# Setting back a planner's count of owed vector work: a two-layer Hyena and attention trunk on one core

## The chip, the core and the metric

The kernel runs on one core of a Trainium2 chip. Its engines are TensorE (PE in the profile, PEld for its weight loads), VectorE (DVE), ScalarE (ACT), GpSimd (POOL) and SyncE (SP, which only issues loads here). The metric is the device time of one execution in microseconds (us), as the median of several runs of the same program.

## The reference

Two layers. Each is a feed-forward, a mixer and another feed-forward, with a residual around each part:

```python
x = x + 0.5 * swiglu(rms_norm(x, ffn1_norm[l]), ...)
h = rms_norm(x, mix_norm[l])
x = x + hybrid_mixer(h, ...)
x = x + 0.5 * swiglu(rms_norm(x, ffn2_norm[l]), ...)
```

x is 256 positions by 1024 channels in float32, and a feed-forward is 2688 wide. The mixer has two branches, merged by gates. One is Hyena: three convolved projections of 512 channels, then twice `z = x_o * (k_o (*) z + D_o z)`, where `(*)` is a long convolution done by a Fourier transform and D_o is a skip weight per channel. The filters k_o come from a small network that depends on the layer's weights only, not on x:

```python
hid = jnp.sin(z @ w1 + b1)
hid = jnp.sin(hid @ w2 + b2)
k = (hid @ w3).reshape(L, HY_ORDER, 2, HY_WIDTH)
k = k * jnp.exp(-t * deltas[None])[:, None, None, :]
full = concatenate([k[:, :, 0], zeros, k[:0:-1, :, 1]])
full = full * lax.rsqrt(jnp.sum(full * full, axis=0) + EPS)
return jnp.fft.rfft(full, axis=0)
```

The other branch is attention in three groups of four heads, with a norm of queries and keys.

## The kernel before

**Weights.** Every matmul with weights is done as three products: each operand is split into a rounded part and the rest. A weight chunk is 128 rows by 1024 float32 (512 KB). `loads` (line 137) lets SP fetch it into one of four `raw` buffers, `pump_hi` (145) lets ACT round it into `whi`, and `pump_lo` (155) lets DVE write the rest, `wlo` (1024 elements a partition). Seven pairs of `whi` and `wlo` exist. The list `srcs` (from line 105) holds the chunks in the order of their use, and SP's queue issues them in that order.

**Slots.** The whole program is written out in one order by hand, and each engine does its part of it in that order. The unit is a slot (236): the matmuls of one weight chunk, usually 24 of 256 columns. Before them a slot lets side work go (`tick`, 211) and flushes what the slot before left (`retire`, 171: a new rounding on ACT, the evacuation if one is due, a new `wlo` on DVE).

**Side work** is written as Python generators that stop at `yield`: the filters and, in layer 0, tables of constants during the first feed-forward; the query and key norms, Hyena and attention during the mixer. A tick takes steps of them as long as the count `owed` is under the stage's room. `ROOM` gives 0.9 for the convolution's slots of the mixer, 2.2 and 2.5 for its later ones, and 1.5 for the feed-forwards. A step that yields True has started something that must come back from another engine. It may go on only when the count at that moment, at most 4.86, has run down to 0.2 (`await_`, 208). The transposes of the convolution (`trans`) and of an opening's result (`turn`) stand in a list of their own, `urgent`, under the same due time but without the room.

**The count** stands for DVE work that is written but not done. Each counted DVE operation adds 0.07 and 1.04e-3 for each element of a partition, and each slot takes off 2.43:

```python
def counted(f):
    def g(**kw):
        owed[0] += OVER + 1.04e-3 * math.prod(kw["out"].shape[1:])
        return f(**kw)
...
def passed(t):
    owed[0] = max(0.0, owed[0] - t)
```

So a `wlo` adds 1.135, an operation on 512 elements 0.602 and one on 256 elements 0.336. The groups at a stage's end and the first half of an opening don't call `passed`.

**Stages.** Each layer has three stages that begin with an `opening` (351). It does four weight chunks first for the even positions (j=0), beside the norm of the odd ones, and then again as four slots for j=1. There are six in all. After it, the first feed-forward runs chunks m=2 to m=20, two slots each (gate and up), with three `acc` banks of PSUM; the evacuation of a chunk is a tanh on ACT and three DVE operations. Then `proj_out` (374) follows. The mixer's opening is followed by six convolution chunks (`conv`, two slots each), the rest of the queries, keys and values, eight gates of two slots, and four merges.

**The filters** (547): a matmul `s<-fc`, a sine (seven DVE operations and an ACT sine), a second matmul `s<-sd`, a second sine, then `st`. For each of the two filters the generator then sets `want` and waits for `fw3_unit` (533), which the feed-forward calls behind chunk m of `FW3`: eight matmuls of the third weights on `st`. If the generator isn't there yet, `fw3_unit` takes its steps one after the other with no matmuls between (`drain`, 248). What follows a unit is one chain: `k`, `sq`, transposes of `sq` and of `rb`, the factor `nb`, the skip row, `hl`, a Fourier matmul, `spec`.

**The first query norm** (`qknorm`, 866) of the mixer: a square on ACT and a reduce on DVE for each half, a scale `ss` on DVE, a power on POOL (`rs`), the product `qk` by `rs` on DVE, and four transposes on PE for each half.

Of the kernel before, what the change touches and what calls it, by code (L numbers as in the profile page):

```python
# [37 lines left out]
ROOM = (0.9, 2.2, 2.5, 1.5, 1.5)  # L38
OVER = 0.07
MARGIN = 0.2  # L40
UNIT = 2.43
DEFER = 4
LEAD = 1
FW3 = (10, 20)


@with_exitstack
def hybrid_trunk(ctx: ExitStack, tc: tile.TileContext, a: dict, out: bass.AP):
# [4 lines left out]
    owed = [0.0]  # L53
# [17 lines left out]
    def nm(s):  # L71
        cnt[0] += 1
        return f"{s}_{cnt[0]}"
# [4 lines left out]
    def f32(t):  # L78
        return t.bitcast(F32)
# [26 lines left out]
    for l in range(NL):  # L106
        def ffn_w(w):
            for i in range(4):
                srcs.append((a[f"gx{w}"][l, i], DM))
            for m in range(2, MF):  # L110
                for g in range(2):
                    srcs.append((a[f"gu{w}"][l, m - 2, g].rearrange("p k c -> p (k c)"), DM))
                if w == 1 and m in FW3:
                    o = FW3.index(m)
                    srcs.append((a["fw3"][l][:, o * DM:(o + 1) * DM], DM))
# [39 lines left out]
    def pump_lo(lead=0):  # L155
        v = ptr["lo"]
        if v >= ptr["hi"] - lead:
            return False
        n = srcs[v][1]
        hi, lo = pairs[v]  # L160
        TT(out=lo[:, :n], in0=raws.pop(v)[:, :n], in1=f32(hi)[:, :n], op=ALU.subtract)
        ptr["lo"] += 1
        loads()
        return True

    def pump(n=99, lead=0):
        loads()
        while n > 0 and (pump_hi() | pump_lo(lead)):
            n -= 1
# [18 lines left out]
    def use():  # L188
        v = ptr["use"]
        ptr["use"] += 1  # L190
        return v
# [7 lines left out]
    def step(g):  # L199
        c = next(g, "end")  # L200
        if c == "end":
            due.pop(g, None)
            return c
        if c:
            await_(g)
        return bool(c)

    def await_(g):
        due[g] = min(owed[0], 2 * UNIT)

    def tick(room):
        for g in list(urgent):
            if due.get(g, 0.0) <= MARGIN and step(g) == "end":
                urgent.remove(g)
        live = [g for g in side if due.get(g, 0.0) <= MARGIN]
        while live and owed[0] < room:
            for g in list(live):
                c = step(g)
                if c == "end":
                    side.remove(g)  # L220
                if c:
                    live.remove(g)
                if owed[0] >= room:
                    break

    def passed(t):
        owed[0] = max(0.0, owed[0] - t)
        for g in due:
            due[g] -= t

    def flush():
        if pend:
            done, evac = pend.pop()
            retire(evac, done)

    def slot(fn, w, done=1, evac=None, room=0.0):
        if pend and getattr(pend[0][1], "first", False):
            flush()
        if room:
            tick(room)  # L240
        flush()
        while ptr["lo"] <= w:
            pump_lo()
        fn(*pairs[w])
        passed(UNIT)
        pend.append((done, evac))

    def drain(ended, room):

        while not ended():  # L250
            tick(room)
            passed(1.0)
# [98 lines left out]
    def opening(acc, evac, n):  # L351

        us = [use() for _ in range(4)]
        per = n // P

        def part(i, j):
            g, k = divmod(i, per)
            return xstat({j: acc[j][g]}, k, n, (j,), g * n if acc[j][0] is acc[j][-1] else 0, j == 0 and i > 1)

        for i in range(4):  # L360
            while ptr["lo"] <= us[i]:
                pump(1)
            part(i, 0)(*pairs[us[i]])
            if i in FEAT1:
                features(1, i - FEAT1[0])()
            for _ in range(FILL[i]):
                pump(1)
        evac(0)
        for i in range(4):
            u = us[i]  # L370
            slot(part(u - us[0], 1), u, evac=(lambda: evac(1)) if i == 3 else None)


    def proj_out(nk, lhs, coef, gain, tags=("x", "acc", "acc", "acc")):
# [71 lines left out]
    def ffn(l, w, gain, chains=()):  # L446
        with tc.tile_pool(name=nm("ffn"), bufs=1, reuse_waits="tile") as fp:
# [66 lines left out]
            for m in range(2, MF):  # L514
# [7 lines left out]
                slot(wstat(pb, sls[1]), use(), evac=evac(m)(pb), room=ROOM[3])  # L522
                if w == 1 and m in FW3:
                    fw3_unit(FW3.index(m))
            drain(lambda: not gens or "dec" in fstate, ROOM[3])
# [21 lines left out]
    def filters(l):  # L547
        def gen(fp):
# [47 lines left out]
            for o in range(2):  # L596
                fstate["want"] = o
                while o not in fstate:
                    yield True
                bs = fstate.pop(o)  # L600
                yield True
                sd, kd = {}, {}
                for j in range(2):
                    for d in range(2):
                        k = fp.tile([P, HW], F32, tag=f"k{j}{d}", name=nm("k"))
                        TT(out=k, in0=bs[j, d], in1=dec[:, j, :], op=ALU.mult)
                        if j == 0 and d == 1:
                            counted(lambda out: dve.memset(out, 0.0))(out=k[0:1, :])
                        kd[j, d] = k
                        yield False  # L610
                if o == 1:
                    fstate["dec"] = True

                sq = gbp.tile([P, HW], F32, tag="sq", name=nm("sq"))
                for n, (j, d) in enumerate(kd):
                    b = bank("s") if n else sq
                    act(out=b, in_=kd[j, d], func=AF.Square)
                    sd[j, d] = sdt(f"{j}{d}")
                    TT(out=sd[j, d], in0=kd[j, 0], in1=kd[j, 1], op=ALU.subtract if d else ALU.add)
                    yield True  # L620
                    if n:
                        TT(out=sq, in0=sq, in1=b, op=ALU.add)
                        yield False

                def halves(j, src):
                    hl = [fp.tile([P, HW], F32R, tag=f"k{j}{d}", name=nm("hl")) for d in range(2)]
                    act(out=hl[0], in_=src, func=AF.Copy)
                    return hl, lambda: TT(out=hl[1], in0=src, in1=f32(hl[0]), op=ALU.subtract)

                yield True  # L630
                yield True
                b = bank("s")
                transpose4(b, [sq[:, c * P:(c + 1) * P] for c in range(4)])
                v = fp.tile([P, 4], F32, tag="v", name=nm("v"))
                r = fp.tile([P, 4], F32, tag="r", name=nm("r"))
                counted(dve.tensor_reduce)(out=v, in_=b.rearrange("p (c t) -> p c t", c=4), axis=mybir.AxisListType.X,
                                           op=ALU.add)
                TS(out=v, in0=v, scalar1=EPS, scalar2=None, op0=ALU.add)
                pool.tensor_tensor(out=r, in0=v, in1=mhalf[:, :4], op=ALU.pow)
                yield True  # L640
                rb = fp.tile([P, 4, P], F32, tag="k00", name=nm("rb"))
                act(out=rb, in_=r.rearrange("p (c o) -> p c o", o=1).to_broadcast([P, 4, P]), func=AF.Copy)
                yield True
                b = bank("s")
                transpose4(b, [rb[:, c, :] for c in range(4)])
                nb = fp.tile([P, HW], F32, tag="k01", name=nm("nb"))
                act(out=nb, in_=b, func=AF.Copy)
                yield True
                for i in range(2):
                    for j in range(2):  # L650
                        t = sd[j, i]
                        TT(out=t, in0=t, in1=nb, op=ALU.mult)
                        if j == 0:
                            TT(out=t[0:1, :], in0=t[0:1, :], in1=sk[:, o, :], op=ALU.add)
                        yield False
                for i in range(2):
                    hls, lates = zip(*[halves(j, sd[j, i]) for j in range(2)])
                    yield True
                    for late in lates:
                        late()  # L660
                        yield late is lates[1]
                    yield True
                    fr = []
                    for j in range(2):
                        b = bank("s")
                        q = 2 * j + i
                        three(b, dft[0][:, q, :], dft[1][:, q, :], *hls[j], True, True)
                        fr.append(b)
                    e = sd[0, i]
                    act(out=e, in_=fr[0], func=AF.Copy)  # L670
                    for g, op in ((0, ALU.add), (1, ALU.subtract)):
                        TT(out=spec[:, o, 2 * g + i, :], in0=e, in1=fr[1], op=op)
                        yield g
# [558 lines left out]
```

## Time and profile before

| | |
|---|---|
| median of three runs | 1120.11 us (1118.97 to 1120.43) |
| the profiled execution, its own time | 1119.33 us |
| span in its trace | 1117.5 us |
| granted TensorE clock, mean of the span | 0.999 of full speed |
| PE busy | 1102.4 us, 99% |
| DVE busy | 840.2 us, 75% |
| ACT busy | 643.3 us, 58% |
| POOL busy | 64.4 us, 6% |

Times in a trace count from the span's start. A row of a timeline gives the start, the duration of the merged instructions, the engine, the line, the operation, what it writes and reads, and how many there are. In brackets stands how long the engine was idle before it and what ended that. A matmul's end is modelled, so the starts are what to go by.

### The profile page before, as it was taken

To read this page: it belongs to the slowest core of one execution; us is meant where nothing else is said; L and a number is where in the kernel's file an instruction comes from. 1 tells how busy PE (TensorE), PEld (TensorE's weight loads), DVE (VectorE), ACT (ScalarE), POOL (GpSimd) and SP (SyncE) were. 2 spreads that over 40 slices of the span, in tenths; PEclk is the share of its full clock that TensorE was granted. 3 is DMA by queue.
4 is the path that set the end of the run, shared out by engine and by line. 5 is a ranking of instruction groups with operands and counts; after the bars stand their busy time and mean duration, and the time that the engine had idled before them with its cause. 6 is when DMAs were issued, how large, how long until landed. Compare 5 with 4: busy or idle time off the path is not lost.

```text
span 1117.5 us, 19195 instructions
## 1 busy us (share of the span) xinstructions
PE 1102.4 (99%) x7591; PEld 1029.3 (92%) x7591; DVE 840.2 (75%) x1243; ACT 643.3 (58%) x983; POOL 64.4 (6%) x113
## 2 busy tenths in 40 slices
PE   9999999999999999999999999999999999999998
PEld 8999988998999999998899998889989998999997
DVE  6779896788865877777567789868888667777772
ACT  6566754665655556666456665547565554666651
POOL 5100000011200000000000000001012000000000
PEclk9999999999999999999999999999999999999999
DMA  8756666556433746667746665737465245666671
GB/s 302 234 168 210 201 212 184 170 171 189 150 115 108 234 140 201 195 193 235 252 147 201 192 209 174 244 110 240 156 185 156 86 125 205 200 192 193 189 256 64
DMA packets 58845, 206.35 MB, mean 185 GB/s; under 512 B 7058, under 2 KB 7718, under 8 KB 58756
## 3 DMA queue, kind: packets, MB, share of 16 engines
q1 hardware_dynamic: 57764, 203.10, 57.3%
q0 software_dynamic: 704, 1.97, 0.6%
q8 instruction: 59, 0.97, 0.4%
q14 instruction: 30, 0.25, 0.1%
q10 hardware_dynamic: 288, 0.07, 0.0%
HBM read 204.00 MB, written 1.11 MB: 184 GB/s over the span
## 4 chain that ended last, share of the span: by engine, by line
PE 82%; DVE 8%; DMA 5%; ACT 3%; issue 2%; POOL 0%; SPq 0%; ACTq 0%; DVEq 0%; POOLq 0%
PE acc L89 54%; PE x L89 13%; PE s L89 12%; DMA raw<-in_gu 4%; DVE wlo L58 3%; PE x L102 2%; DVE spec L58 1%; ACT whi L151 1%; DVE t L58 1%; DVE xn L58 1%; ACT sq L285 1%; DVE x L58 1%; DVE hT L58 1%; PE x L750 1%; PE s L102 0%
## 5 line engine op out<-in xcount | busy, mean ns | idle before, releaser
L58 DVE TENSOR_TENSOR wlo<-raw,whi 128x1024 fp32r<-128x1024 f32 (+1 forms) x380 | 457.6, 1210 | 54.8 <-ACT whi L151 54.5
L151 ACT ACTIVATE whi<-raw 128x1024 fp32r<-128x1024 f32 (+1 forms) x380 | 392.8, 1046 | 142.3 <-PE acc L89 52.6
L89 PE MATMUL acc<-hT,whi 128*128 128x256 f32 (+1 forms) x2416 | 463.5, 290 | 0.0
L89 PEld LDWEIGHTS acc<-hT,whi 128*128 128x128 f32 x2416 | 379.6, 192 | 8.2 <-issue 1.3
L89 PE MATMUL acc<-hT,wlo 128*128 128x256 f32 x1360 | 367.1, 275 | 0.0
L89 PEld LDWEIGHTS acc<-hT,wlo 128*128 128x128 f32 x1360 | 260.9, 192 | 1.9
L89 PE MATMUL acc<-whi,hid 128*128 128x512 f32 (+1 forms) x378 | 115.5, 357 | 0.0
L89 PE MATMUL acc<-whi,hT 128*128 128x256 f32 (+1 forms) x576 | 115.2, 328 | 0.0
L89 PE MATMUL x<-whi,hid 128*128 128x512 f32 x336 | 112.1, 380 | 0.0
L89 PE MATMUL s<-hT,whi 128*128 128x512 f32 x304 | 104.0, 383 | 0.0
L89 PEld LDWEIGHTS acc<-whi,hT 128*128 128x128 f32 x576 | 88.0, 191 | 8.6 <-ACT hT L317 1.1
L89 PEld LDWEIGHTS acc<-whi,hid 128*128 128x128 f32 x378 | 71.0, 189 | 8.6
L89 PE MATMUL s<-hT,wlo 128*128 128x256 f32 x304 | 76.7, 273 | 0.0
L89 PEld LDWEIGHTS x<-whi,hid 128*128 128x128 f32 x336 | 63.6, 189 | 7.9
L89 PE MATMUL acc<-wlo,hid 128*128 128x512 f32 (+1 forms) x189 | 66.4, 356 | 0.0
L89 PEld LDWEIGHTS s<-hT,whi 128*128 128x128 f32 x304 | 57.7, 190 | 6.9 <-DVE c L58 0.7
L89 PE MATMUL acc<-wlo,hT 128*128 128x256 f32 (+1 forms) x288 | 63.4, 324 | 0.4 <-DVE wlo L58 0.2
L89 PE MATMUL x<-wlo,hid 128*128 128x512 f32 x168 | 63.7, 379 | 0.0
L481 ACT ACTIVATE hid<-t 128x256 fp32r<-128x256 f32 x38 | 19.9, 523 | 70.1 <-DVE t L58 70.1
L89 PEld LDWEIGHTS s<-hT,wlo 128*128 128x128 f32 x304 | 58.1, 191 | 1.9
L58 DVE TENSOR_TENSOR hid<-t,hid 128x256 fp32r<-128x256 f32 x76 | 35.5, 466 | 22.4 <-ACT hid L481 22.4
L58 DVE SCALAR_TENSOR_TENSOR t<-t,acc 128x256 f32<-128x256 f32 x46 | 19.2, 417 | 43.0 <-ACT t L457 33.1
(189 smaller groups left out, 1297.4 us busy)
## 6 DMA issues: line engine op xcount, KB each, us to landing
raw<-in_gu SPq DMA_DIRECT2D x152, 512.0 KB, 4.3
raw<-in_dn SPq DMA_DIRECT2D x84, 512.0 KB, 4.4
raw<-in_win_q SPq DMA_DIRECT2D x32, 512.0 KB, 4.0
raw<-in_wg SPq DMA_DIRECT2D x32, 512.0 KB, 4.2
raw<-in_win_h SPq DMA_DIRECT2D x24, 512.0 KB, 4.5
raw<-in_gx SPq DMA_DIRECT2D x16, 512.0 KB, 5.0
raw<-in_wo SPq DMA_DIRECT2D x16, 512.0 KB, 4.1
raw<-in_wp SPq DMA_DIRECT2D x16, 384.0 KB, 3.0
```

What stands on the lines that cost most here:

```text
L58: return f(**kw)
L89: nc.tensor.matmul(o, l, r, start=start, stop=stop)
L102: nc.tensor.transpose(b[:, q * P:(q + 1) * P], ap, ident)
L151: act(out=pairs[v][0][:, :n], in_=raws[v][:, :n], func=AF.Copy)
L285: act(out=sq, in_=x[:, j, sl], func=AF.Square, scale=1.0 / 32.0, accum_out=nst[j][:, h:h + 1])
L481: act(out=hi, in_=tv, func=AF.Copy)
L750: nc.tensor.transpose(tb[j][:, (q0 + i) * P:(q0 + i + 1) * P], c[:, i, 1 + j:1 + S:2], ident)
```

## The change

An opening now ends by setting the count to at most 2.0. The first third-layer weights of the filters are loaded and used behind m=8 and not m=10. The skip row is added to the sum of the two filter sides only (`i == 0`, the even part) and not to their difference. The difference goes into sine terms, which are 0 at that position.

```diff
 MARGIN = 0.2
+OPEN = 2.0
 UNIT = 2.43
...
-FW3 = (10, 20)
+FW3 = (8, 20)
...
             slot(part(u - us[0], 1), u, evac=(lambda: evac(1)) if i == 3 else None)
+        owed[0] = min(owed[0], OPEN)
...
                         TT(out=t, in0=t, in1=nb, op=ALU.mult)
-                        if j == 0:
+                        if j == 0 and i == 0:
                             TT(out=t[0:1, :], in0=t[0:1, :], in1=sk[:, o, :], op=ALU.add)
```

## Rows read from the trace of the kernel before

**Rows 1.** The page's first part, PE's line with its neighbours: busy us, share, instructions.
```profile
PE 1102.4 (99%) x7591; PEld 1029.3 (92%) x7591; DVE 840.2 (75%) x1243; ACT 643.3 (58%) x983; POOL 64.4 (6%) x113
```

**Rows 2.** Waits of PE: us in total, times, the longest.
```profile
PE s L89 <- DVE hl L58: 2.3, 2, 1.4
PE x L89 <- ACT at L939: 1.5, 2, 0.8
PE s L102 <- DVE sq L58: 1.5, 1, 1.5
PE s L102 <- ACT rb L642: 1.2, 2, 1.0
PE x L89 <- DVE st L58: 1.2, 1, 1.2
...
PE s L89 <- ACT sd L578: 0.6, 1, 0.6
...
PE s L89 <- DVE spec L58: 0.3, 2, 0.2
```

**Rows 3.** The chain that ended last, seven slots of layer 0's feed-forward: start, us.
```profile
112.83 18.76 PE acc L89 x168
```

**Rows 4.** Timeline of PE, first feed-forwards: start of m=2, first filter matmul, both layers.
```profile
22.57 0.39 PE L89 MATMUL acc<-hT,whi 128*128 128x256 f32 x2
...
44.54 0.70 PE L89 MATMUL s<-fc 33*128 33x256 f32 x2
...
577.04 0.39 PE L89 MATMUL acc<-hT,whi 128*128 128x256 f32 x2
...
599.01 0.70 PE L89 MATMUL s<-fc 33*128 33x256 f32 x2
```

**Rows 5.** Timelines of ACT and DVE, layer 0: evacuations of m=5 and m=6, a sine.
```profile
50.53 0.36 ACT L457 ACTIVATE t<-acc 128x256 f32<-128x256 f32 x1
...
56.26 0.42 ACT L578 ACTIVATE sd<-sd 128x256 f32<-128x256 f32 x1 [1.67 <-DVE sd L58]
...
58.93 0.38 ACT L457 ACTIVATE t<-acc 128x256 f32<-128x256 f32 x1
...
59.35 0.42 DVE L58 SCALAR_TENSOR_TENSOR t<-t,acc 128x256 f32<-128x256 f32 x1 [3.12 <-ACT t L457]
```

**Rows 6.** Timelines of ACT, DVE, POOL and PE in layer 0's mixer, first query norm.
```profile
218.71 1.00 ACT L770 ACTIVATE c<-acc,cw 128x256 f32<-128x256 f32 x2
219.80 1.66 DVE L58 SCALAR_TENSOR_TENSOR c<-acc,cw,c 128x256 f32<-128x256 f32 x4 [1.56 <-ACT c L770]
221.14 0.61 ACT L871 ACTIVATE sq<-qk 128x512 f32<-128x512 f32 x1
...
224.12 0.66 PE L750 MATMUL x<-ident,c 128*128 128x128 f32 x4
...
227.43 0.68 DVE L58 TENSOR_REDUCE ss<-sq 128x8 f32<-128x512 f32 x1
228.14 0.18 DVE L58 TENSOR_SCALAR ss<-ss 128x16 f32<-128x16 f32 x1
228.25 1.23 DVE L58 TENSOR_TENSOR wlo<-raw,whi 128x1024 fp32r<-128x1024 f32 x1
228.40 3.84 POOL L877 TENSOR_TENSOR rs<-ss,mhalf 128x16 f32<-128x16 f32 x1 [26.33 <-DVE ss L58]
...
233.84 0.68 DVE L58 TENSOR_TENSOR qk<-qk,rs 128x512 f32<-128x512 f32 x1
...
240.31 0.60 PE L102 MATMUL x<-ident,qk 128*128 128x128 f32 x4
```

**Rows 7.** Timelines of POOL and DVE in layer 0's mixer, third query norm.
```profile
291.95 2.90 POOL L877 TENSOR_TENSOR rs<-ss,mhalf 128x16 f32<-128x16 f32 x1 [14.93 <-DVE ss L58]
...
294.88 0.69 DVE L58 TENSOR_TENSOR qk<-qk,rs 128x512 f32<-128x512 f32 x1 [0.51 <-POOL rs L877]
```

**Rows 8.** Timeline of DVE, layer 0's first feed-forward: a skip row.
```profile
117.81 0.68 DVE L58 TENSOR_TENSOR sd<-sd,sk 1x512 f32<-1x512 f32 x1
```

## The prediction

> **What bounds the kernel now.** I read the page's first part, then the PE waits, then the order of time around the six openings. PE is busy 1102.4 of 1117.5 us [rows 1], and the change takes no matmul away. So the time can only move through PE's waits, and those of the filter chains and the mixers are few [rows 2]: by what PE waited for, 2.3 for hl, 1.5 for at, 1.5 for sq, 1.2 for rb, 1.2 for st, 0.6 for the sine's sd, 0.3 for spec. Seven groups, 8.6 us in both layers. All but at belong to the filter chain (7.1 us). A change of the order can give back at most these, and can add new ones wherever PE meets an operation before DVE or ACT has made its input. That second half decides here.
>
> The clock of the walk is the slot: 168 matmuls, seven slots, took 18.76, so a slot is 2.68 [rows 3] where the planner credits 2.43.
>
> **The change part by part.**
>
> *The count.* An opening leaves the count high because its weight splits are counted at 1.135 each and only half of its matmuls are credited. From the code: entering chunk m=2 with X, slot by slot the count moves by -0.62, -1.30, -0.29, -1.30, +0.32, -1.30, -0.29, -1.30 (a split 1.135, an evacuation 1.01, the turn's split 0.60, less 2.43). The first filter matmul comes in the ninth slot in both layers (44.54 after a start at 22.57, 599.01 after 577.04) [rows 4]. With room 1.5 that needs X between 6.3 and 7.6. In the mixer the same sum with room 0.9 (-1.30, -1.30, +0.05, -1.30) and the first square in the fifth slot (221.14) [rows 6] gives X between 3.4 and 4.7. All are above 2.0, so the edit acts in four of the six openings; in the second feed-forwards no side work waits, and the turn's due time gives the same slot with 2.0 as with its cap of 4.86.
>
> *First feed-forward of each layer.* With 2.0 the first filter matmul moves from the ninth slot to the second (1.38 is under 1.5), seven slots or 18.8 us earlier. The sine's second matmul comes in the sixth or seventh slot, st in the tenth. The first filter weights, at m=8, are used after the fourteenth: four slots to spare, so the 1.2 for st goes, and the 0.6 for sd, as its sine is two slots or more behind. From there the first filter's chain (k's, sq, two transposes, nb, halves) needs 23 slots, and its last spec lands in the tick of the first slot of m=20. So the unit at m=20 need not drain it: the 2.3 for hl and the 0.3 for spec, both from the forced end, go. Together -4.4.
>
> What stays: the transposes still follow sq by two slots and rb by one, so the 2.7 for sq and rb stays as a sum. Bounds: 0 and 5.0 (layer 1 as bad as layer 0).
>
> What comes: the tanh of an evacuation runs behind PE. Chunk m=5 ended at 44.5, where the ninth slot opens, and its tanh began at 50.53, 6.0 behind; m=6 ended at 50.5 and its tanh, behind a sine that waited 1.67 for DVE, began at 58.93, 8.4 behind [rows 5]. So a sine adds 2.4. There are three acc banks, so a bank must be free two chunks (10.7) after its end, and tanh plus two DVE operations take 1.3 (0.42 to the first and 0.42 for each) [rows 5]: PE waits beyond 9.4 behind. The two sines, now three slots apart, leave no chunk between to recover: 6.0 + 2 x 2.4 = 10.8, a wait of 1.4 a layer. Bounds 0 (no such row before) and 2.8 for both; I take 1.0 each, +2.0, near the upper end, as the early slots are the late ones.
>
> *The mixers.* Call the convolution's slots 0a, 0b, 1a, 1b, ... From the transposes of the first c, which open 2b at 224.12 [rows 6], 0a begins at 210.7 and 2a at 221.44. With 2.0 the count is 0.71 at 0b, so the first query norm runs then: square in 0b, its reduce and second square in 1a, second reduce and scale in 1b, the product with rs in 2a, its transposes in 2b. Before, the square was in 2a, the product in 4a and the transposes opened 5a at 240.31 [rows 6], so everything had passed when PE came. The transposes of the first c also move from 2b to 2a, since their due time falls to 0.13, under the margin 0.2.
>
> Now the walk. c is written by ACT at 218.71 and its taps run from 219.80 to 221.46. Two squares of 0.61 now stand ahead of c on ACT; I take a third of their 1.2, 0.4, as delay, since DVE idled 1.56 for c, a sign that ACT was waiting there too. Taps end at 221.86: PE, at 2a since 221.44, waits 0.5. Reduce 0.6 and scale (0.18) follow: 222.6. POOL takes 3.84 for rs: 226.6. The product (0.68) ends at 227.4. PE has reached 2b at 221.95 + 0.4 + 2.68 = 225.0: it waits 2.4. Behind the product on DVE stand a split (1.23), four taps (1.66) and the second product, 3.6 in all, while PE has 3.1 of work: 0.45. Sum 3.35 a mixer, 6.7 for both. What else queues behind that product on DVE, the weight splits, is some chunks ahead and hides. Before, 5.6 us lay between scale (228.14) and product (233.84) [rows 6], so nothing shows the wait; the nearest is the third norm, where the product followed POOL's end at 294.85 with DVE idle 0.51 [rows 7]. There POOL took 2.90. Bounds for both mixers: 4.0 (POOL 2.90 and no delay by the squares) and 8.4 (all of their 1.2).
>
> The 3.84 has a split beside it that began 0.15 before POOL (228.25); the 2.90 has none [rows 6, 7]. The Trainium skill, SBUF — State Buffer, section "Who interferes with whom", says that a VectorE instruction with two SBUF inputs and a GpSimd instruction that reads SBUF exclude each other, the first to issue holding the interface to its end. The trace agrees: 0.94 more where 1.08 of the split was left. The scale is again followed by a split, so by the rule 3.84 holds, which speaks against this change; by 2.90 the sum would be 1.9 lower.
>
> *The mixers' end.* With the query norm done early, Hyena is two products (1.2 of the count, about one slot) ahead. The 1.5 for at comes from the last attention heads, forced after the last gate. One slot sooner could remove it; the steps are whole slots, so I take half, -0.8. Bounds 0 and -1.5.
>
> *The skip term.* Four additions of one row by 512 go, 0.68 each [rows 8]. DVE is 75% busy [rows 1] and PE's work covers them: 0. Without that cover they would be 2.7. Their count, 0.60 a filter, is what lets the chain just fit into m=20.
>
> *The weights of the first filter.* One load of 512 KB stands two chunks earlier on SP's queue, four others one place later, each used as much later. The skip row's load moves with st. Nothing waits longer: 0.
>
> **The sum.** -4.4 + 2.0 + 6.7 - 0.8 = +3.5. The profiled execution took 1119.33 for its span of 1117.5, so 1122.8; it lies 0.8 under the median of the three runs, 1120.11, so 1123.6 for the median.
>
> **The rivals.** All for the median; 0.2% (2.24 us) is about what a measurement of this kernel can tell from no change.
>
> - *The query norm's result is there in time* (faster). If the scale ends 2.4 earlier in the mixer, by 220.2, its transposes do not wait. For it: ACT and DVE idle before c (1.56) [rows 6], so earlier weights would pull c forward. Against: c itself is written at 218.71, and the taps stand ahead of the scale. Then -4.4 + 2.0 - 0.8: 1116.9. Chance 0.10.
> - *The early start clears all of the filter's waits* (faster). If DVE catches up in the idle slots between st and m=8, sq and rb go too and no bank is late: -7.1 + 4.0 - 0.8: 1116.2. Against: the lag was 6.0 before any sine. Chance 0.10.
> - *They cancel*: mixers at their least, 4.0: +0.8, so 1120.9. Chance 0.17.
> - *Nothing happens*, because the count is below 2.0 anyway: 1120.1. The slots of rows 4 and 6 exclude it nearly. Chance 0.02.
> - *Dearer*: layer 1's sq and rb as late as layer 0's (+2.3), banks 2.8, mixers 8.4: +9.1, so 1129.2. Chance 0.06.
>
> **How the numbers follow.** The forecast has 0.55, and its own range is 1121.5 to 1128; a little of it (0.04) lies within 0.2%. Faster: 0.10 + 0.10 = 0.20. Within: 0.17 + 0.02 + 0.04 = 0.23. Slower: 0.57. The range reaches from between the two faster cases to just under the dearest: 1116.5 to 1129.
>
> **What would show it.** Right: s<-fc near 25.3 and near 580; PE waits for st, hl and spec gone; an idle PE at a transpose of qk near 225 and 774, released by DVE qk, with POOL's rs just before and lasting some 3.8; a short wait at the first c's transposes. A wait on an acc bank near m=7 would show the two sines. Wrong: qk's transposes without idle time, or sq and rb gone in both layers. The steps I trust least are the bank wait and the delay by the squares; the order itself follows from the count.

## The result: 0.7% slower, lost in the mixers

The changed kernel took 1127.96 us (median of 4 runs, 1124.32 to 1130.58), the kernel before 1120.27 beside it (1118.97 to 1120.71, 4 runs): ratio 1.0068, 95% interval 1.0039 to 1.0098. It is slower, as forecast, but by 7.7 where 3.5 was forecast: 4.4 more than the 1123.6 forecast, inside the range of 1116.5 to 1129, and only 0.04 under the upper end of the forecast's own, 1121.5 to 1128. The profiled execution took 1124.32 for a span of 1122.5, which is 5.0 more than before; the other three runs lie 3.3 to 6.3 above it, and what follows has to account for both differences.

The page's first part after, to be read beside [rows 1]:

```profile
PE 1103.0 (98%) x7591; PEld 1031.6 (92%) x7591; DVE 838.7 (75%) x1239; ACT 642.5 (57%) x983; POOL 62.3 (6%) x113
```

DVE has four instructions fewer (the skip rows), PE the same 7591 matmuls. The time is in the gaps. PE's waits after (us in total, times, the longest), which answer to [rows 2]:

```profile
PE x L103 <- DVE qk L59: 3.6, 2, 2.3
PE x L103 <- ACT at L936: 3.3, 2, 1.6
PE s L103 <- DVE sq L59: 3.3, 2, 1.7
PE acc L90 <- DVE t L59: 1.1, 1, 1.1
...
PE s L103 <- ACT rb L644: 0.9, 2, 0.6
...
PE x L752 <- DVE c L59: 0.2, 1, 0.2
```

hl, st, sd and the filter's spec are gone from the list, 4.4 us of [rows 2]. New are qk, c and the acc bank; at has doubled and sq with rb has grown from 2.7 to 4.2.

Where this lies is best read by stage. I cut both spans at the same PE instructions: the start of m=2, a matmul in the mixer's opening (in layer 0 at 204.56 before and at 201.69 after), the last transpose at the mixer's end, in both layers, and the end. Columns: stretch, its length, PE busy and matmuls, the granted clock, the DMA share, GB/s. The kernel before:

```profile
22.57:204.56 181.99, 176.53 (x1264) 1.00 0.62 196
204.56:358.66 154.10, 153.07 (x1162) 1.00 0.51 159
358.66:577.04 218.38, 217.95 (x1329) 1.00 0.62 196
577.04:754.64 177.60, 175.77 (x1265) 1.00 0.60 192
754.64:908.74 154.10, 153.07 (x1162) 1.00 0.52 160
908.74:1117.50 208.76, 205.12 (x1280) 1.00 0.57 183
```

The changed kernel:

```profile
22.51:201.69 179.18, 175.64 (x1264) 1.00 0.63 199
201.69:361.09 159.40, 155.14 (x1162) 0.99 0.49 156
361.09:578.81 217.72, 217.29 (x1330) 1.00 0.61 196
578.81:756.58 177.77, 175.65 (x1265) 1.00 0.60 191
756.58:913.77 157.19, 153.68 (x1161) 1.00 0.50 158
913.77:1122.50 208.73, 205.09 (x1280) 1.00 0.58 182
```

The first feed-forwards gained 2.81 and lost 0.17; the two mixers lost 5.30 and 3.09; the stretch between the layers gained 0.66 and the tail is the same. That is the whole +5.0. In the mixers PE stands 4.26 and 3.51 where it stood 1.03, and it is also longer busy with the same matmuls, by 2.07 in layer 0 and 0.61 in layer 1.

The first query norm of layer 0's mixer after, on ACT, DVE, POOL and PE, to be read beside [rows 6]:

```profile
213.31 0.62 ACT L873 ACTIVATE sq<-qk 128x512 f32<-128x512 f32 x1
...
219.69 0.18 DVE L59 TENSOR_SCALAR ss<-ss 128x16 f32<-128x16 f32 x1
219.77 1.22 DVE L59 TENSOR_TENSOR wlo<-raw,whi 128x1024 fp32r<-128x1024 f32 x1
219.94 3.82 POOL L879 TENSOR_TENSOR rs<-ss,mhalf 128x16 f32<-128x16 f32 x1 [20.75 <-DVE ss L59]
223.79 0.69 DVE L59 TENSOR_TENSOR qk<-qk,rs 128x512 f32<-128x512 f32 x1 [2.80 <-POOL rs L879]
224.63 1.06 PE L103 MATMUL x<-ident,qk 128*128 128x128 f32 x4 [2.27 <-DVE qk L59]
```

The chain runs without a slot to spare: the scale ends at 219.87, POOL needs 3.82, DVE stands 2.80 for it, and PE, which had been there since 222.36, stands 2.27. Before, 11.9 us lay between POOL's start and these transposes. The four transposes then took 1.06, where 0.60 is usual [rows 6], and so did what followed: the granted clock had fallen. Windows of PE after:

```profile
220.00:225.00 5.00, 2.73 (x24) 0.97 0.35 107
225.00:230.00 5.00, 5.00 (x34) 0.69 0.40 110
```

A mean of 0.69 is a mixture of the two levels, 1.2 and 2.4 GHz; the run with one slot more, below, has a window of 5 us at 0.50. In the kernel before no window of 5 us is below 1.00 until PE has ended.

Layer 1 shows the same chain with a shorter POOL (POOL, DVE and PE):

```profile
774.98 2.91 POOL L879 TENSOR_TENSOR rs<-ss,mhalf 128x16 f32<-128x16 f32 x1 [20.89 <-DVE ss L59]
775.16 1.23 DVE L59 TENSOR_TENSOR wlo<-raw,whi 128x1024 fp32r<-128x1024 f32 x1 [0.26 <-issue]
...
778.77 0.63 PE L103 MATMUL x<-ident,qk 128*128 128x128 f32 x4 [1.36 <-DVE qk L59]
```

Here POOL began 0.18 ahead of the split and not behind it, took 2.91 and not 3.82, and PE's wait is 1.36 and not 2.27. Both are shorter by the same 0.91, so PE's wait follows POOL's time.

At the mixer's end (ACT and PE, layer 0) the last attention head is scored behind the last gate, its exponential ends at 358.15, and PE stands 1.64 for it, about twice the 0.76 of before. There a gate's matmuls stood behind the last scores, and only the copy of the transposed head was late. Before and after:

```profile
357.17 1.10 PE L89 MATMUL x<-v,at 128*128 128x64 f32 x8 [0.76 <-ACT at L939]
```

```profile
355.45 1.11 PE L90 MATMUL x<-qkT,odd 128*128 128x128 f32 x8
...
357.34 0.72 ACT L936 ACTIVATE at<-at,mx 128x512 f32<-128x512 f32 x1 [1.01 <-DVE mx L59]
...
358.20 0.66 PE L103 MATMUL x<-ident,at 128*128 128x128 f32 x4 [1.64 <-ACT at L936]
```

And the second sine of layer 0's first feed-forward, on ACT, DVE and PE, which answers to [rows 5]:

```profile
44.85 1.28 ACT L580 ACT_TABLE_LOAD   x1
...
48.55 0.42 ACT L580 ACTIVATE sd<-sd 128x256 f32<-128x256 f32 x1 [2.42 <-DVE sd L59]
48.88 1.04 ACT L152 ACTIVATE whi<-raw 128x1024 fp32r<-128x1024 f32 x1
49.94 1.28 ACT L459 ACT_TABLE_LOAD   x1
51.23 0.38 ACT L459 ACTIVATE t<-acc 128x256 f32<-128x256 f32 x1
...
52.67 0.46 PE L90 MATMUL acc<-hT,whi 128*128 128x256 f32 x2 [1.12 <-DVE t L59]
```

### The profile page after: what moved, and what is told of

The parts are those of the page before. It is cut to its first block, busy times and chain, and to the rows that moved or that the text cites. A ratio compares the mean times of both kernels' runs of the same rounds, so it can differ in the third digit from the quotient of the medians.

```text
span 1122.5 us, 19202 instructions
## 1 busy us (share of the span) xinstructions
PE 1103.0 (98%) x7591; PEld 1031.6 (92%) x7591; DVE 838.7 (75%) x1239; ACT 642.5 (57%) x983; POOL 62.3 (6%) x113
## 4 chain that ended last, share of the span: by engine, by line
PE 75%; DVE 10%; DMA 6%; ACT 5%; issue 3%; POOL 1%; ACTq 0%; SPq 0%; DVEq 0%; POOLq 0%
PE acc L90 48%; PE x L90 13%; PE s L90 12%; DMA raw<-in_gu 4%; DVE wlo L59 4%; ACT whi L152 2%; PE x L103 2%; DVE t L59 1%; DVE sd L59 1%; DMA raw<-in_win_h 1%; DVE spec L59 1%; POOL rs L879 1%; ACT L459 0%; ACT t L459 0%; PE x L752 0%
## 5 line engine op out<-in xcount | busy, mean ns | idle before, releaser
L90 PEld LDWEIGHTS acc<-wlo,hT 128*128 128x128 f32 x288 | 45.1, 190 | 5.4 <-DVE wlo L59 1.9
```

What stands on the lines that cost most here:

```text
L90: nc.tensor.matmul(o, l, r, start=start, stop=stop)
```

## The experiments

The theory: the loss is made in the mixers, where the query norm now starts too early for POOL, with a lower clock behind PE's waits; the feed-forward part is a small gain. The rivals: the feed-forward part carries the loss; the low count lets all side work run ahead of DVE, wherever the norm stands; the clock falls by itself. The runs below come from three chips, numbered 8, 14 and 4, with the kernel before beside them on each: 1117.79, 1117.49 and 1118.04 (17, 23 and 23 runs). So kernels are compared by their ratio to it.

**The changed kernel once more** (on chip 14).

> The changed kernel once more, beside the others of this call. By its first four times: ratio 1.0068, clock 0.995 to 0.998, times spread over 4 or more; runs at 0.998 about 3 faster than runs at 0.995.

Measured: 1125.41, ratio 1.0073 (1.0054 to 1.0093), clock 0.995 to 0.998 in all six runs, 1123.61 to 1128.44. The loss is the same on chip 14. The expected order by clock is not there: the run at 0.998 took 1125.19, two at 0.997 took 1123.61 and 1124.16. In this execution's profile the acc bank's wait was 2.84 in place of 1.12, and sq's 0.9 in place of 3.3; with the same program the waits of the filter chain change from one execution to the next, those of the mixers (qk 3.6, at 3.3) do not.

**The count set back in the feed-forwards alone.**

```diff
-        owed[0] = min(owed[0], OPEN)
+        if n == 256:
+            owed[0] = min(owed[0], OPEN)
```

> Changed kernel, but the count is set back only after the openings of the feed-forwards, not of the mixers. Theory (the mixers carry the loss): by the PE waits of the changed kernel the feed-forward part is worth -1.8 (filter waits 7.1 before, 5.3 after with the acc bank's 1.1), and qk, c and the growth at at are gone, so 1118.4 (1117.3 to 1119.6), granted clock of every run 0.999. Rival (the early filter chain or the moved load carries it): 1124 or more. Rival (the clock falls by itself in this kernel): the clock stays at 0.995 to 0.998 and the time over 1122.

Measured, on chip 8 like the next three: 1117.56 (12 runs), ratio 0.9997 (0.9984 to 1.0011). The waits for qk and c are gone, at is back at 1.5, and layer 0's mixer is 154.10 long again. So the loss is in the mixers, and the rival that puts it in the feed-forwards has fallen. But the gain of 1.8 is only at the interval's edge: sq and rb took 5.3 here and the acc bank 1.4. That is 4.0 over the 2.7 of before, about the 4.4 that went with hl, st, sd and spec. The expected clock of 0.999 in every run did not come either: seven of the twelve runs are at 0.997 or 0.998. But the kernel before, beside it, has six of 17 at 0.998, so some falls of the clock belong to the kernel and not to the change.

**The count set back in the mixers alone**, in the kernel before (`if n == 512:`, first filter weights at m=10, old skip term).

> Kernel before with the count set back only after the openings of the mixers; filter weights and skip term as before. Theory: waits for qk 3.6 and c 0.2, at 1.8 longer, and 2 to 4 for PE's lower clock behind them, so 1120.2 + 7.6 to 9.6: 1127.8 to 1129.8, with a granted clock of 0.995 to 0.998. Rival (the feed-forward part carries the loss): 1119.5 to 1121.

Measured: 1126.38, ratio 1.0096 (1.0069 to 1.0122), where 1.0068 to 1.0086 was expected: this part alone makes the whole loss. qk took 4.5, at 3.3 and c 0.7 in this profile (in layer 1, too, POOL began behind the split here, took 3.82, and PE waited 2.27), all at full clock, so its two mixers, 158.61 and 157.82 long, show the price without the clock:

```profile
203.28:361.89 158.61, 153.69 (x1162) 1.00 0.48 157
757.15:914.97 157.82, 153.65 (x1162) 1.00 0.48 157
```

That is 4.5 and 3.7 over 154.10. Of the six runs two were at a clock of 1.0 (1125.46, 1125.53), two at 0.997 and 0.998 (1126.40, 1126.36), and two at 0.992 and 0.991 (1133.47, 1133.13).

**The first filter weights and the skip term without the count.**

```diff
-        owed[0] = min(owed[0], OPEN)
```

> Changed kernel without setting the count back: first filter weights at m=8 and the shorter skip term alone. Theory: the two edits belong together; the first filter matmul stays in the ninth slot, five slots ahead of the unit at m=8 where the chain needs eight, so three slots of the second sine are forced there and PE stands for about 4 a layer, +8, less the 1.8 for st and sd and the 2.6 for hl and spec, as the unit ends four slots sooner: 1123.8 (1121.5 to 1127), no wait for qk. Rival (setting back the count does nothing for the filter chain): like the feed-forward part alone, 1118 to 1119.5.

Measured: 1127.22, ratio 1.0083 (1.0068 to 1.0099). The two edits do belong together. The price is +0.83%, over twice the 3.6 us expected: PE stood 10.9 for st, 5.96 and 4.90, where I had put 4 a layer, and all six runs had a clock of 0.992 to 0.994. Nothing waited for sq, rb or hl here. The first of PE's two waits for st, on PE's timeline:

```profile
68.70 0.79 PE L90 MATMUL x<-whi,st 128*128 128x512 f32 x1 [5.96 <-DVE st L59]
```

**One slot more between POOL's rs and the product**, first query norm only.

```diff
                                    in1=mhalf, op=ALU.pow)
                 yield True
+                if blk == 0:
+                    yield True
```

> Changed kernel with one more slot between POOL's rs and the product in the first query norm of each mixer. Theory: POOL's 3.82 is the late part, so the waits for qk (3.6) and the lower clock behind them (2 to 4) go, the wait at the mixers' ends (at) stays at 3.3: 1121.5 to 1124, granted clock 0.998 or more. Rival (DVE is behind altogether there, the wait moves along to the next transposes): 1127 to 1129. Rival (the clock falls for another reason): qk's wait is gone but the clock stays at 0.995 to 0.998, 1124 to 1126.

Measured: 1125.68, ratio 1.0071 (1.0052 to 1.0089), a clock of 0.994 or 0.995 in four of the six runs: no gain, and here the theory as I had put it fell. The first norm no longer waits, but the second does, and PE's waits for qk sum to 3.8 in four places. DVE, POOL and PE in layer 0's second norm:

```profile
274.80 0.17 DVE L59 TENSOR_SCALAR ss<-ss 128x16 f32<-128x16 f32 x1
275.05 3.28 POOL L879 TENSOR_TENSOR rs<-ss,mhalf 128x16 f32<-128x16 f32 x1 [50.56 <-DVE ss L59]
278.36 0.69 DVE L59 TENSOR_TENSOR qk<-qk,rs 128x512 f32<-128x512 f32 x1 [1.03 <-POOL rs L879]
...
279.20 0.63 PE L103 MATMUL x<-ident,qk 128*128 128x128 f32 x4 [1.66 <-DVE qk L59]
```

The wait has moved along, as the rival said, but not because DVE is behind: DVE itself stood 1.03 for POOL. It is the same late part in another place. PE was at these transposes 2.5 after POOL's start, one slot; in the changed kernel's first norm 2.4 (layer 0). In the changed kernel's second norm 5.6 lay between POOL's start (276.42) and the transposes (282.04), and nothing waited. So what counts is how many slots the walk happens to leave between scale and transposes, of each norm, and one is too few. This run can't say whether the norm's early start or the low count brings that about. The next one can.

**The count set back everywhere, the first query norm at its old place.**

```diff
             def qknorm(blk, qk):
...
+                for _ in range(3 if blk == 0 else 0):
+                    yield True
                 for j in range(2):
```

> Changed kernel, count set back after all openings, but the first query norm of each mixer lets three slots go by before its first square, so that it starts in the fifth slot as before. Theory (it is the norm's early start that costs: POOL's rs is late for it): no wait for qk, the waits at the mixers' ends back to 0.8, each mixer 154.1 long, time as with the count set back in the feed-forwards alone, 1117.6 (1116 to 1119). Rival (the low count itself lets all side work run ahead of DVE, as when one slot more was left behind rs and the waits moved to the second norm): waits for qk or c of 1.5 to 2.5 a mixer elsewhere, at still 1.6, 1121 to 1125.

Measured, on chip 4 like the run with the old skip term below: 1117.85 (12 runs), ratio 1.0001 (0.9988 to 1.0014). Three slots of patience take the whole loss away. There is no wait for qk or c, at is at 0.76 in both layers, and the mixers are as long as before:

```profile
202.77:357.00 154.23, 153.21 (x1161) 1.00 0.50 160
753.08:907.18 154.10, 153.08 (x1162) 1.00 0.49 159
```

So it is the norm's early start, and not the low count, that costs; the rival has fallen. This run also settles at: its growth hangs on the norm's place as well.

**Matmuls put where PE stands**, in the changed kernel: 18 ahead of the first query norm's transposes, 14 ahead of those of the first filter's sq and of attention's last head. Their products are overwritten.

```diff
+    def fill(b, n):
+        for _ in range(n):
+            mm(b[:, :S], hT[:, 0, 0, 0, :], hT[:, 0, :, 0, :], True, True)
...
+                if o == 0:
+                    fill(b, 14)
                 transpose4(b, [sq[:, c * P:(c + 1) * P] for c in range(4)])
...
+                    if blk == 0 and j == 0:
+                        fill(b, 18)
                     transpose4(b, [qk[:, j, q * P:(q + 1) * P] for q in range(4)])
...
+                    if n == 7:
+                        fill(b, 14)
                     transpose4(b, [at[n][:, q * P:(q + 1) * P] for q in range(4)])
```

> Changed kernel with matmuls of 256 columns put where PE stands: 18 ahead of the transposes of the first query norm, 14 ahead of those of the first filter's sq, 14 ahead of those of attention's last head; they write the bank that the transposes then overwrite, and nothing uses them. They shorten no wait of the data: at 0.112 each they fill 2.0 and 1.6. Theory (the clock falls behind a stretch in which PE stands): every run has a clock of 0.999 or 1.0 and all lie within 2 of each other, at the changed kernel's time at full clock, 2 to 3 under its median in this call, although PE has more to do. Rival (the clock falls for another reason, or costs nothing): median and clock as those of the changed kernel, 0.995 to 0.998, or up to 1 longer by the overfill.

Measured, on chip 14 like the skip term alone and the better version: 1124.70, ratio 1.0065 (1.0048 to 1.0082), beside 1125.41 for the changed kernel. Five of the six runs had a clock of 0.999 or 1.0, and lay within 2 (1123.83 to 1125.77); the changed kernel had none above 0.998. PE got 10 us more to do (2 x 46 x 0.112) and the kernel became no slower. The sixth run, the profiled one, shows why not all: the acc bank's wait, which I had not filled, was 2.56 there, and behind it the clock fell (PE, windows):

```profile
50.00:55.00 5.00, 2.44 (x20) 0.94 0.12 48
55.00:60.00 5.00, 5.00 (x35) 0.72 0.61 200
```

So the clock falls behind stretches in which PE stands. The expected 2 to 3 of gain came out as 0.7, inside the noise of six runs; the fill was also longer than the waits wherever those were short (sq 0.9 in the changed kernel's profile on this chip, against 3.1 of fill). The run shows that filling the waits takes most falls away; what a fall costs it does not show.

**The skip term alone**, in the kernel before (`if j == 0 and i == 0:`).

> Kernel before with the skip term on the even part alone. Prediction's step: the two additions a layer that go lie under PE's work, so 0: ratio 0.999 to 1.001. Rival (their count lets the chain end a slot sooner, so the wait for hl shrinks): 1 to 2.6 faster, ratio 0.9977 to 0.999.

Measured: 1116.42 (12 runs), ratio 0.9989 (0.9977 to 1.0001). Zero is just inside the interval, and the point lies in the rival's range (0.9977 to 0.999), just outside the prediction's (0.999 to 1.001). In the profile hl waits 0.5 in place of 2.3, in layer 1 not at all, which is the rival's mechanism; its size can't be told from nothing.

**The feed-forward part with the old skip term** (count set back for n == 256, m=8, skip on both parts).

> Count set back after the openings of the feed-forwards alone and the filter weights at m=8, but the skip term added on both parts as before. Prediction's step (its count is what lets the chain just fit into m=20): the waits for hl and spec come back, 1.5 to 2.6, 1119 to 1121.5 beside 1117.6 with the short skip term. Rival (the seven slots won carry the chain in any case): no wait for hl, 1117 to 1118.5.

Measured: 1117.23 (12 runs), ratio 0.9999 (0.9986 to 1.0013), and no wait for hl or spec. The prediction's step that the shorter skip term lets the chain just fit has fallen; the slots won at the start suffice.

**A better version**: the count set back in the feed-forwards alone, the filter weights one chunk sooner still, and the two slots so won given to the two waits that had stayed.

```diff
-FW3 = (8, 20)
+FW3 = (7, 20)
...
-        owed[0] = min(owed[0], OPEN)
+        if n == 256:
+            owed[0] = min(owed[0], OPEN)
...
                 yield True
                 yield True
+                if o == 0:
+                    yield True
                 b = bank("s")
                 transpose4(b, [sq[:, c * P:(c + 1) * P] for c in range(4)])
...
+                if o == 0:
+                    yield True
                 b = bank("s")
                 transpose4(b, [rb[:, c, :] for c in range(4)])
```

> Count set back only after the openings of the feed-forwards, as in the run of that part alone, but the first filter weights one chunk sooner still (m=7), and the two slots so won are given to the first filter's chain: one more ahead of the transposes of sq and one ahead of those of rb. Theory (sq and rb are late by less than a slot): their 3.8 and 1.5 go, and the falls of the clock behind them; against the 1115.6 of that run's times at full clock 1110 to 1112.5, ratio to before about 0.995. Rival (st is now late at m=7): a wait for st of 1 to 4 in each layer, 1114 to 1118. Rival (DVE stays behind, the waits move along to nb and the halves): 1115 to 1118.

Measured: 1115.12 (12 runs, 1114.20 to 1117.01), ratio 0.9978 (0.9968 to 0.9988): faster than the kernel before, by about half of what was expected, and 10 us under the changed kernel on the same chip. The gain is not one of clock alone: the five runs at 1.0 took 1115.19 in the median, the 12 such runs of the kernel before 1117.07. Nothing waits for sq or st; of rb one wait of 1.7 stays (layer 0):

```profile
PE s L103 <- ACT rb L647: 1.7, 1, 1.7
```

## Why the prediction was right, and where it was not

- **The count and the order** came as worked out. The first filter matmuls stand at 25.29 and 581.58 (25.3 and some 580 were named), and the edit acted in four of the six openings.
- **First feed-forwards, -4.4**: st, sd, hl and spec are gone, all of it. **The acc bank, +2.0**: 1.1 in the profiled execution, layer 0 alone, at the chunk that was named; 2.8 in the second profile, 0.7 to 2.6 in the experiments that keep this part, and once in layer 1 too.
- **"The 2.7 for sq and rb stays"** was off: 4.2 after, and 2.5 to 5.3 in the other profiles with this chain (those with fills left out), which is the bounds' 0 to 5.0 and a little over. By stages the feed-forwards gave -2.6 where -2.4 was forecast, but the runs of this part alone (0.9997 and 0.9999) show no gain: in their profiles sq, rb and the acc bank took 6.2 to 6.7, where the filter chain's waits had been 7.1 before.
- **The query norm in the mixer, +6.7**: right in kind and place, mis-sized in the first profile. qk at j=0 was 2.27 and 1.36 (2.4 forecast for each), j=1 nothing (0.45), c 0 and 0.24 (0.5): 3.9 in all; the second profile has 4.8 and the run of the mixers alone 5.3. In layer 0 POOL's rs took 3.82 with a split of 1.22 beside it, as priced; in layer 1 it took 2.91, which is 0.91 of the 2.8 by which the term was too large. Of the Trainium skill, SBUF — State Buffer, section "Who interferes with whom", whose exclusion of such a pair the prediction had weighed, layer 0 bears out that a POOL that issues second is held up. Layer 1 does not bear out the reverse: by that rule the split, which issued 0.18 behind POOL, would have stood until POOL's end at 777.89, but it took its usual 1.23 from 775.16. So 3.82 was not sure; it hung on which of the two began first. Two slips in the walk are small: 226.6 and 0.68 make 227.3, not 227.4, and the 1.56 before c is idle time of DVE alone, as ACT came to c straight from a rounding.
- **The mixer's end, -0.8**: the step that failed, with the wrong sign. At took 3.28 in place of 1.52, +1.8, outside the bounds 0 to -1.5. I had taken Hyena's lead for a gain of the whole walk. But the slots are as many as before, and what one chain takes earlier another gets later. The third norm's second transposes and attention's first scores came at 304.61 and 310.40, 102.9 and 108.7 after the start of the mixer's stretch, where they had come 95.9 and 101.7 after it (the scores below, before and after). PE's own delay until then, its wait of 2.27 and the lower clock behind it, is some 4 of these 7; the rest is a slot. In the run of the mixers alone, at full clock, the scores came 107.9 after that start, and with the norm at its old place 101.9. Attention ends as many rounds after its start as before, so one round more falls behind the last gate, where nothing covers it. That the early norm does it is shown (it goes with the norm at its old place); that Hyena is what takes the slots is argued from the order alone.

```profile
306.30 1.06 PE L89 MATMUL x<-qkT,qkT 128*128 128x128 f32 x8
```

```profile
310.40 1.06 PE L90 MATMUL x<-qkT,qkT 128*128 128x128 f32 x8
```

- **What no step had: the clock.** Layer 0's mixer lost 5.30, of which waits explain 4.26 - 1.03 = 3.2 and the longer busy time 2.1. Not all of that is the clock: at full clock, in the run of the mixers alone, PE is 0.6 longer busy too, which leaves some 1.5 for the fall. The mixers sum to +8.4 where +5.9 was forecast, but at full clock to +8.2 (4.5 and 3.7). So what the forecast missed there is not the clock first: at came to +1.8 for -0.8, and no term stood for the 0.6 of busy time in each mixer.
- **The skip term, 0**: within the interval of its run, though its point (-0.11%) fits the rival better. **The load, 0**: no wait for a filter weight appears after.

Right, then, because the sign hung on the mixers' term, which held in kind; the size owes something to luck. In the profiled mixers qk and c cost 2.8 less than forecast and at 2.6 more, and 2.7 of longer busy time had no term; the median stayed in the forecast's own range by 0.04. Five us of the profiled execution are accounted for stage by stage. The 2.7 by which the median rose further lie in executions without a trace; the lower clocks (0.995 to 0.997) and the changing wait for the acc bank speak for these two together, and how they share it stays open.

## What to carry to other kernels

When a planner's credit is corrected, every generator that lives on it moves, not only the one that was short of slots; look for those whose inner distances (here scale, POOL, product, transposes) were safe only because the walk was slow. A chain with a long step on a slow engine needs its distance written into it: three slots put there took away the whole loss of 0.7%. In a walk with a fixed number of slots, work that comes earlier pushes other work later, so ask which chain now ends last.

## What the runs showed of the hardware

The price of a wait of PE is not its length alone: behind one the granted clock may fall. In layer 0's mixer it did so after a wait of 2.27 in the changed kernel, and did not after the same wait of 2.27 in the run of the mixers alone, nor in the second profile of the changed kernel itself. There the same mixer took 158.54 in place of 159.40, although its first c cost a wait of 0.68 besides:

```profile
203.16:361.70 158.54, 153.69 (x1161) 1.00 0.48 157
```

So it is not certain at any one wait; in executions it shows as a spread. The twelve profiles of this study hold 13 such falls ahead of PE's end (windows of 5 us), each at or just behind a wait of PE of 0.76 or more; the kernel before, the mixers alone and the norm at its old place have none. The stretch after the last mixer, the same 1280 matmuls each time, gives a price for one fall. The changed kernel's second profile, and the better version's, in which the clock fell at its start, just behind waits of 0.76 and 0.26 among short matmuls:

```profile
914.65:1123.40 208.75, 205.10 (x1280) 1.00 0.55 182
```

```profile
902.56:1113.00 210.44, 206.74 (x1280) 0.99 0.56 182
900.00:905.00 5.00, 3.98 (x24) 0.76 0.57 205
905.00:910.00 5.00, 5.00 (x42) 0.90 0.35 105
```

1.7 us, more than the waits that brought it. Over all twelve profiles this stretch took 208.7 to 208.8 in the seven without a fall there, and 210.0 to 210.4 in the five with one. The kernel before has these waits too (at, in [rows 2]), and on chip 14 eleven of its 23 runs are at 0.997 or 0.998; their median is 1119.24, that of the twelve at 1.0 is 1117.07.

The second: a sine between tanhs costs ACT two table loads of 1.28 each (44.85 and 49.94), 2.56 in all, near the 2.4 of lag for a sine that I had read from [rows 5]. The Trainium skill, ScalarE: Activation LUTs, section "What ACT_TABLE_LOAD costs", gives 1283 ns for the load, and the trace agrees; it adds a drain of about 1380 ns to every switch, and this trace shows none: the load at 49.94 follows a split that ends at 49.92, and the tanh starts at 51.23, where the load ends.
